# Rotation of 96 images by 90 degrees on one core: the last 16 MB of the loads move from SyncE's DMA queue to ScalarE's

## The chip, the core and the metric

The kernel runs on one core of one Trainium2 chip. The metric is the device time of one execution in microseconds (us). The core has compute engines of which two work here: VectorE (DVE in the profile) and ScalarE (ACT). SyncE (SP) computes nothing; it issues DMA transfers. Every transfer is cut up over the core's 16 DMA engines, whichever engine issued it.

## The reference

```python
def setup_inputs():
    batch, c, h, w = 32, 3, 256, 256
    return {"x": np.random.randn(batch, c, h, w).astype(np.float32)}

def reference(x):
    return np.rot90(x, k=-1, axes=(-2, -1)).astype(np.float32)
```

There are 96 images of 256 x 256 float32 numbers, and each is turned clockwise: row r of an image becomes a column. Nothing is calculated. 25.17 MB are read, 25.17 MB are written, and in between the numbers change places.

## The kernel before

All the data fit into the on-chip memory at once. They are split into five groups of 2, 2, 2, 4 and 2 slabs (`sizes`). One slab holds 128 partitions x 4096 numbers, that is 2048 KB, and in this text 1 MB is 1024 KB. Each group has one buffer `u0` to `u4` (all called u in the profile), in which its data are loaded, turned in place, and stored from. The whole kernel is straight-line code, and the order of the Python text is the order on each engine, as far as the waits between engines matter.

**Loads.** SyncE issues 14 of them, all on its one queue. They are numbered here from 0 in the order of issue:

- loads 0 and 1 (L55, 1 MB each) and load 2 (L56, 2 MB) bring group 0;
- loads 3 and 4 (L66, 2 MB each) bring group 1;
- loads 5 and 6 (L66) bring group 2;
- loads 7 to 10 (L66) bring group 3;
- load 11 (L66, 2 MB), load 12 (L63, 1 MB, named `mark`) and load 13 (L64, 1 MB) bring group 4.

The framework guards the transfers with eight semaphores, used in turn. So the issue of load k + 8 waits until load k has landed.

**Turning.** For each group VectorE makes transposes of 128 x 2048 numbers: L72 for group 0, and L88 and L93 for the others. A quarter or half of each group goes aside into `spare` or `extra` (L72, L88) while the rest moves inside u (L93). Then ScalarE copies the part that went aside back into u: two copies at L78 for group 0, and two to eight at L98 for each of the other groups. `turn_group` of group n needs all loads of that group.

**Stores.** SyncE issues ten of them, numbered here from 0: stores 0 and 1 (L106) for group 0, and two for each other group (L113): stores 2 and 3, 4 and 5, 6 and 7 (group 3, 4 MB each), 8 and 9. All others have 2 MB. A written-out dependence makes store 0 wait until load 12 (`mark`) has landed, so that practically all of the reading comes before all of the writing; the other stores follow on SyncE in order. Each waits for ScalarE's last copy of its group.

Functions that the change touches:

Of the kernel before, what the change touches and what calls it, by code (L numbers as in the profile page):

```python
# [1 line left out]

# [4 lines left out]


@with_exitstack  # L10
def kernel(
    ctx: ExitStack,
    tc: tile.TileContext,
    x: bass.AP,
    out: bass.AP,
):

    nc = tc.nc
    fp32 = mybir.dt.float32

    B, C, H, W = x.shape
    P = nc.NUM_PARTITIONS
    R = 16  # L30
    E = R * W
    hw = R // 2
    low, high = slice(0, hw), slice(hw, R)

    rows_in = x.rearrange("b c h w -> (b c h) w")
    rows_out = out.rearrange("b c h w -> (b c h) w")

    sizes = (2, 2, 2, 4, 2)
    first = [sum(sizes[:n]) for n in range(len(sizes))]
    groups = [  # L40
        ctx.enter_context(tc.tile_pool(name=f"group{n}", bufs=1)).tile([P, s, E], fp32, name=f"u{n}")
        for n, s in enumerate(sizes)
    ]
    psum = ctx.enter_context(tc.tile_pool(name="psum", bufs=1, space=bass.MemoryType.PSUM))
    spare = [psum.tile([P, E // 2], fp32, name=f"spare{h}") for h in range(2)]
    extra = ctx.enter_context(tc.tile_pool(name="extra", bufs=1)).tile([P, E // 2], fp32, name="extra")

    def rows_of(rows, n):
        return rows[first[n] * P * R : (first[n] + sizes[n]) * P * R]


    ld = rows_of(rows_in, 0).rearrange("(s i p r) w -> s i p (r w)", s=2, i=2, p=P)
    home = [groups[0][:, s].rearrange("p (i f) -> p i f", i=2) for s in range(2)]
    for i in range(2):
        nc.sync.dma_start(out=home[0][:, i], in_=ld[1, i])  # L55
    nc.sync.dma_start(out=home[1], in_=ld[0].transpose([1, 0, 2]))  # L56
    for n in range(1, len(sizes)):
        I = sizes[n]
        ld = rows_of(rows_in, n).rearrange("(a i m r) w -> i m a (r w)", a=2, i=I, m=P // I)
        to = groups[n].rearrange("p s f -> p (s f)").rearrange("p (a f) -> p a f", a=2)  # L60
        for i in range(I):
            if (n, i) == (len(sizes) - 1, I - 1):
                mark = nc.sync.dma_start(out=to[i::I, 0], in_=ld[i][:, 0])  # L63
                nc.sync.dma_start(out=to[i::I, 1], in_=ld[i][:, 1])  # L64
            else:
                nc.sync.dma_start(out=to[i::I], in_=ld[i])  # L66

    def turn_slab(src, dsts):
        s = src.rearrange("p (i r g c) -> p c r g i", i=2, r=R // 2, c=R)
        for h, d in enumerate(dsts):  # L70
            d = d.rearrange("p (c k r) -> p c r k", c=hw, r=R // 2)[:, :, ::-1, ::-1]
            nc.vector.transpose(out=d, in_=s[:, h * hw : (h + 1) * hw])  # L72

    u = groups[0]
    turn_slab(u[:, 0], spare)
    turn_slab(u[:, 1], [u[:, 0, : E // 2], u[:, 0, E // 2 :]])
    for h in range(2):
        nc.scalar.copy(out=u[:, 1, h * E // 2 : (h + 1) * E // 2], in_=spare[h])  # L78

    def turn_group(n, held):  # L80
        I = sizes[n]
        T = I // 2
        K = W // (R * T)
        u = groups[n].rearrange("p s f -> p (s f)")
        src = u.rearrange("p (a t r g c) -> p t c r g a", a=2, t=T, r=R, c=R)
        dst = u.rearrange("p (i c k t r) -> p t c r k i", i=I, c=R, k=K, t=T)[:, ::-1, :, ::-1, ::-1, :]
        for t in range(T):
            nc.vector.transpose(  # L88
                out=held[t].rearrange("p (i c k r) -> p c r k i", i=I, c=hw, k=K)[:, :, ::-1, ::-1, :],
                in_=src[:, t, low, low])  # L90
        for c, r in ((low, high), (high, high), (high, low)):
            for t in range(T):
                nc.vector.transpose(out=dst[:, t, c, r], in_=src[:, t, c, r])  # L93
        back = u.rearrange("p (i c k t r) -> p t i c k r", i=I, c=R, k=K, t=T)[:, ::-1]
        for t in range(T):
            kept = held[t].rearrange("p (i c k r) -> p i c k r", i=I, c=hw, k=K)
            for i in range(I):
                nc.scalar.copy(out=back[:, t, i, low, :, high], in_=kept[:, i])  # L98

    for n, held in enumerate(([extra], [spare[1]], spare, [extra]), 1):  # L100
        turn_group(n, held)


    st = rows_of(rows_out, 0).rearrange("(s i m r) w -> i m s (r w)", s=2, i=2, m=P // 2)
    for a in range(2):
        put = nc.sync.dma_start(out=st[a], in_=groups[0][a::2])  # L106
        if a == 0:
            tc.add_manual_dep(put.ins, mark.ins.name, mybir.DependencyInfo(
                mybir.DependencyClass.Sync, mybir.DependencyReason.SCHED_ONLY), reason="stores after loads")
    for n in range(1, len(sizes)):  # L110
        st = rows_of(rows_out, n).rearrange("(a i m r) w -> a m i (r w)", a=2, i=sizes[n], m=P // 2)
        for a in range(2):
            nc.sync.dma_start(out=st[a], in_=groups[n][a::2])  # L113


# [1 line left out]
_INS = ['x']  # L117
_OUTS = [((32, 3, 256, 256), 'float32')]


# [23 lines left out]
```

## Time and profile before

| | |
|---|---|
| median of 3 runs | 123.02 us (122.89 to 123.17) |
| the profiled execution | 122.88 us |
| its span in the profile | 121.1 us |
| VectorE busy | 87.4 us (72%), 24 instructions |
| ScalarE busy | 14.9 us (12%), 17 instructions |
| DMA | 50.33 MB (of a million bytes), mean 416 GB/s over the span |
| DMA queues in use | one (q1, from SyncE): 3456 packets, 97.6% of the 16 DMA engines' span |

The profile's times count from the start of the span. 1.78 us of the profiled execution lie outside of the span. A DMA issue is an instruction of its own on the issuing engine's sequencer (SPq for SyncE, ACTq for ScalarE); the profile gives the time it takes there, and apart from this the time from issue until the data have landed. The trace also keeps a record for each packet that a DMA engine moves: its start, its length and its size. Most packets here have 16 KB and there is one small packet at the end of each transfer on each DMA engine, which reports the landing.

### The profile page before, as it was taken

What the parts mean: (1) busy time and instruction counts of PE and PEld (TensorE: products, weight loads), DVE (VectorE), ACT (ScalarE), POOL (GpSimd) and SP (SyncE); (2) the same over time, 40 slices, a digit from 0 to 9 for tenths busy, and PEclk for the clock granted to TensorE, in tenths of its full rate; (3) what the DMA queues carried; (4) which work ended last, traced back from release to release, by engine and by line L of the source; (5) the groups of instructions that cost most, each with busy time, mean ns of one, the idle gap of its engine ahead of it and who ended that gap; (6) DMA issues with size and microseconds to landing.
All of it is one profiled execution on the core that took longest, in us unless ns stands there. A gap on an engine that the chain in (4) does not pass through costs nothing.

```text
span 121.1 us, 131 instructions
## 1 busy us (share of the span) xinstructions
DVE 87.4 (72%) x24; ACT 14.9 (12%) x17; POOL 0.2 (0%) x4
## 2 busy tenths in 40 slices
DVE  0039999999999999999999999999999600000000
ACT  0000400380005100060000000318000330000000
POOL 0000000000000000000000000000000000000000
DMA  2999999999989898999999999999999999999994
GB/s 89 428 428 422 452 433 433 433 433 433 520 346 520 346 520 346 428 422 411 433 433 428 433 433 428 417 417 433 428 433 433 433 433 433 433 433 433 433 422 184
DMA packets 3456, 50.33 MB, mean 416 GB/s; under 512 B 384, under 2 KB 384, under 8 KB 384
## 3 DMA queue, kind: packets, MB, share of 16 engines
q1 hardware_dynamic: 3456, 50.33, 97.6%
HBM read 25.17 MB, written 25.17 MB: 416 GB/s over the span
## 4 chain that ended last, share of the span: by engine, by line
DVE 66%; issue 6%; DMA 6%; ACT 1%; ACTq 1%; SPq 0%; DVEq 0%
DVE u L93 39%; DVE spare L88 9%; DVE extra L88 6%; DVE u L72 6%; DVE spare L72 6%; DMA u<-in_x_dram 6%; ACT u L98 1%; ACTq L139 1%; SPq L55 0%; DVEq L88 0%; DVEq L72 0%
## 5 line engine op out<-in xcount | busy, mean ns | idle before, releaser
L93 DVE STREAM_TRANSPOSE u<-u 128x2048 f32<-128x2048 f32 x15 | 54.4, 3649 | 0.4
L72 DVE STREAM_TRANSPOSE spare<-u 128x2048 f32<-128x2048 f32 x2 | 7.1, 3586 | 8.1 <-DMA u<-in_x_dram 8.1
L98 ACT COPY u<-spare 128x512 f32<-128x512 f32 (+1 forms) x10 | 6.0, 687 | 38.5 <-DVE u L93 38.5
L88 DVE STREAM_TRANSPOSE spare<-u 128x2048 f32<-128x2048 f32 x3 | 10.7, 3588 | 0.0
L72 DVE STREAM_TRANSPOSE u<-u 128x2048 f32<-128x2048 f32 x2 | 7.8, 3988 | 0.0
L88 DVE STREAM_TRANSPOSE extra<-u 128x2048 f32<-128x2048 f32 x2 | 7.8, 3896 | 0.0
L98 ACT COPY u<-extra 128x1024 f32<-128x1024 f32 x4 | 4.0, 1043 | 22.8 <-DVE u L93 22.8
L78 ACT COPY u<-spare 128x2048 f32<-128x2048 f32 x2 | 3.6, 1870 | 8.7 <-DVE u L72 8.7
L78 ACT ACT_TABLE_LOAD x1 | 1.3, 1283 | 13.0 <-DMA u<-in_x_dram 13.0
L128 POOL MEMSET const-uint8-127<- 128x1 uint8 x1 | 0.1, 103 | 0.0
L128 POOL MEMSET const-bfloat16-1.0<- 128x1 bf16 x1 | 0.1, 102 | 0.0
L128 POOL MEMSET const-float32-0.0<- 128x1 f32 x1 | 0.1, 99 | 0.2 <-issue 0.2
L128 POOL MEMSET const-float32-1.0<- 128x1 f32 x1 | 0.1, 99 | 0.0
## 6 DMA issues: line engine op xcount, KB each, us to landing
u<-in_x_dram SPq DMA_DIRECT2D x10, 2048.0 KB, 30.4
out_dram<-u SPq DMA_DIRECT2D x8, 2048.0 KB, 18.2
out_dram<-u SPq DMA_DIRECT2D x2, 4096.0 KB, 21.1
u<-in_x_dram SPq DMA_DIRECT2D x4, 1024.0 KB, 20.5
```

Of the source, the lines that this page charges most:

```text
L72: nc.vector.transpose(out=d, in_=s[:, h * hw : (h + 1) * hw])
L78: nc.scalar.copy(out=u[:, 1, h * E // 2 : (h + 1) * E // 2], in_=spare[h])
L88: nc.vector.transpose(out=held[t].rearrange("p (i c k r) -> p c r k i", i=I, c=hw, k=K)[:, :, ::-1, ::-1, :], in_=src[:, t, low, low])
L93: nc.vector.transpose(out=dst[:, t, c, r], in_=src[:, t, c, r])
L98: nc.scalar.copy(out=back[:, t, i, low, :, high], in_=kept[:, i])
L128: nc = _bacc.Bacc("TRN2", target_bir_lowering=False, num_devices=1)
L139: with _tile.TileContext(nc) as tc:
```

## The change

Loads 0 to 4 (8 MB) are still issued by SyncE. Loads 5 to 13 (16 MB) are put into a list `later` and issued by ScalarE on its own DMA queue. The first of them, load 5, gets a written-out dependence on load 3 (`early`), with which 6 MB have landed; the other eight follow in ScalarE's program order. `keep` fixes that order among the ScalarE instructions: loads 5 to 10, the two copies L78, loads 11, 12 and 13, and then the copies L98 of groups 1 to 4. `mark`, for which store 0 waits, is still load 12. The shapes of the transfers, the work of VectorE and the stores on SyncE stay as they are.

```diff
+    last = {}
+
+    def keep(inst):
+        before = last.get(inst.ins.engine)
+        if before is not None:
+            tc.add_manual_dep(inst.ins, before, ... NoSync, SCHED_ONLY ..., reason="order")
+        last[inst.ins.engine] = inst.ins.name
+        return inst
...
+    later = []
     for n in range(1, len(sizes)):
...
         for i in range(I):
-            if (n, i) == (len(sizes) - 1, I - 1):
-                mark = nc.sync.dma_start(out=to[i::I, 0], in_=ld[i][:, 0])
-                nc.sync.dma_start(out=to[i::I, 1], in_=ld[i][:, 1])
+            if n == 1:
+                got = nc.sync.dma_start(out=to[i::I], in_=ld[i])
+                if i == 0:
+                    early = got
+            elif (n, i) == (len(sizes) - 1, I - 1):
+                later += [(to[i::I, a], ld[i][:, a]) for a in range(2)]
             else:
-                nc.sync.dma_start(out=to[i::I], in_=ld[i])
+                later.append((to[i::I], ld[i]))
+
+    def load(k):
+        for o, i in later[k]:
+            got = keep(nc.scalar.dma_start(out=o, in_=i))
+            if "x" not in last:
+                last["x"] = None
+                tc.add_manual_dep(got.ins, early.ins.name, ... Sync, SCHED_ONLY ..., reason="loads in turn")
+        return got
...
+    load(slice(0, 6))
+
     u = groups[0]
     turn_slab(u[:, 0], spare)
     turn_slab(u[:, 1], [u[:, 0, : E // 2], u[:, 0, E // 2 :]])
     for h in range(2):
-        nc.scalar.copy(out=u[:, 1, h * E // 2 : (h + 1) * E // 2], in_=spare[h])
+        keep(nc.scalar.copy(out=u[:, 1, h * E // 2 : (h + 1) * E // 2], in_=spare[h]))
...
-                nc.scalar.copy(out=back[:, t, i, low, :, high], in_=kept[:, i])
+                keep(nc.scalar.copy(out=back[:, t, i, low, :, high], in_=kept[:, i]))
+
+    mark = load(slice(6, -1))
+    load(slice(-1, None))
```

More of the change, by code (lines that the diff above doesn't have):

```diff
@@ L49, in rows_of @@
         return rows[first[n] * P * R : (first[n] + sizes[n]) * P * R]
+    last = {}
+    def keep(inst):
+        before = last.get(inst.ins.engine)
+        if before is not None:
+            tc.add_manual_dep(inst.ins, before, mybir.DependencyInfo(
+                mybir.DependencyClass.NoSync, mybir.DependencyReason.SCHED_ONLY), reason="order")
+        last[inst.ins.engine] = inst.ins.name
+        return inst
     ld = rows_of(rows_in, 0).rearrange("(s i p r) w -> s i p (r w)", s=2, i=2, p=P)
@@ L61 @@
         for i in range(I):
-            if (n, i) == (len(sizes) - 1, I - 1):
-                mark = nc.sync.dma_start(out=to[i::I, 0], in_=ld[i][:, 0])
-                nc.sync.dma_start(out=to[i::I, 1], in_=ld[i][:, 1])
-            else:
-                nc.sync.dma_start(out=to[i::I], in_=ld[i])
+            if n == 1:
[4 more added lines that the diff above has]
+                later += [(to[i::I, a], ld[i][:, a]) for a in range(2)]
+            else:
+                later.append((to[i::I], ld[i]))
[4 more added lines that the diff above has]
+                last["x"] = None
+                tc.add_manual_dep(got.ins, early.ins.name, mybir.DependencyInfo(
+                    mybir.DependencyClass.Sync, mybir.DependencyReason.SCHED_ONLY), reason="loads in turn")
+        return got
     def turn_slab(src, dsts):
```

## Prediction

> **What bounds the kernel now.** I read the page first, for which resource is full.
>
> ```profile
> span 121.1 us, 131 instructions
> DVE 87.4 (72%) x24; ACT 14.9 (12%) x17; POOL 0.2 (0%) x4
> DMA  2999999999989898999999999999999999999994
> q1 hardware_dynamic: 3456, 50.33, 97.6%
> ```
>
> The only row that is full from edge to edge is DMA: its first slice has 2 tenths and its last has 4. VectorE stops at slice 32 of 40. The chain of waits names VectorE for most of the span, since it follows instructions backwards and ends in a store, but the stores stand in a queue. So I looked at the windows next.
>
> ```profile
> 20.00:40.00 20.00, 19.90 (x6) 5.63 (x4) 0.00 (x0) 1.00 1.01 433
> 40.00:60.00 20.00, 19.86 (x7) 1.93 (x2) 0.00 (x0) 1.00 1.00 430
> 60.00:80.00 20.00, 19.93 (x6) 1.07 (x2) 0.00 (x0) 1.00 1.00 429
> 80.00:100.00 20.00, 15.78 (x5) 5.02 (x8) 0.00 (x0) 1.00 1.00 425
> 100.00:119.00 19.00, 0.00 (x0) 0.00 (x0) 0.00 (x0) 1.00 1.01 428
> ```
>
> The last two columns are DMA share and GB/s: full in the load half (to 60 us), full in the store half, full when VectorE has ended. The trace's packet records say it more sharply. Chained into 16 engines, data packets run from 1.7 to 2.8 us (first ones) until 119.7 to 119.9 us, and no engine has a gap of 0.1 us in between, also not where load 13 gives way to store 0. A packet of 16 KB takes 611 to 619 ns; summed over a DMA engine, all packets together lie 0.80 us above the shortest of their size, 0.20 us of it before 3 us and 0.27 us in the loads from 3 to 60 us.
>
> So the time is 1.78 us outside of the span + about 2.3 us until the engines run + 117.4 us of packets + 1.3 us from the last packet to the end of the span = 122.8 us, against 122.88 us of the profiled execution. That execution lies 0.14 us under the median of 123.02 us, within the scatter of the three runs (0.28 us).
>
> Third view: SP's own waits (us in total, times, longest).
>
> ```profile
> SPq L106 <- DMA u<-in_x_dram: 31.2, 1, 31.2
> SPq L66 <- DMA u<-in_x_dram: 10.4, 3, 4.4
> SPq L113 <- ACT u L98: 5.0, 2, 3.0
> ```
>
> And three of its issues in the timeline (start, length in us).
>
> ```profile
> 17.84 0.61 SPq L66 DMA_DIRECT2D u<-in_x_dram  x1
> 59.43 1.37 SPq L106 DMA_DIRECT2D out_dram<-u  x2
> 84.25 15.73 SPq L113 DMA_DIRECT2D out_dram<-u  x4
> ```
>
> SP waits for its eight semaphores: load 11 goes out at 17.84, when load 3 has landed (17.82 in the trace), loads 12 and 13 at 22.75 and 27.64 when loads 4 and 5 have. All this runs some 30 us ahead of the data. Store 0 goes out at 59.43, when load 12 has landed. Store 6 goes out at 84.25, when group 3 is turned; its data are due only when store 5 is through, at 90.4 us.
>
> Fourth, the chain in order of time around the place that is touched:
>
> ```profile
> 15.18 7.60 DVE u L72 x2
> 22.78 0.06 issue
> 22.84 3.92 DVE extra L88
> ```
>
> VectorE is through with group 0 at 22.78 us, and load 4, which it needs next, landed at 22.73 us. It has no reserve there: every us by which load 4 is later is a us for VectorE, and VectorE never idles again before 95.9 us, so nothing absorbs it.
>
> **The change, part by part.** *Issues.* Nine issues leave SP (613 ns each by the median of L66, about 500 ns for L63 and L64). SP waits over 31 us for load 12 anyhow: no gain. On ScalarE they stand in line with its copies. Six issues from 17.84 on, 6 x 0.61 + 5 x 0.05 = 3.9 us, end at 21.7. The table load (1.28 us, at 13.0 before) may then end at 23.0, where the L78 copies start today (23.03, after VectorE). Copies until 26.7, loads 11 to 13 behind them by about 28.2 (load 13 has to wait for load 5's landing, about 27.6). Loads 5 to 10 last the queue until 51.5 us, and the next copy (L98 of group 1) is due at 37.7 us, so both sides have over 9 us of cover. Cost 0; VectorE needs `spare` back only at 37.6 us.
>
> *The hand-over.* Load 5's issue waits for load 3 (17.82 us). How long does ScalarE's idle queue take until packets move? The nearest row is the start of the kernel: issue at 0.73, first packets on four engines at 1.73 to 1.82 and on the other twelve at 2.39 to 2.79, so 1.0 to 2.06 us. That puts load 5 at 18.8 to 19.9 us. Load 4 alone keeps the engines busy until 22.2 us, 2.3 us longer. Cost 0; without that cover it would be the whole 1.0 to 2.06 us.
>
> *The shared stretch.* From about 19.3 us both queues have packets for every DMA engine. If they alternate one to one, the remaining 2.3 to 3.4 us of load 4 take twice as long. Its data end at 24.5 to 25.6, it lands 0.48 us later (as load 4 does today, 22.24 to 22.73), at 25.0 to 26.1 us, and VectorE is late by 2.2 to 3.3 us from there on. What is late next is store 6: issued at 86.5 to 87.6 instead of 84.25. It must go out 1.6 to 2.1 us (as long as store 0 and the head took) ahead of 90.4, so by 88.3 to 88.8 us: the reserve of 4.1 to 4.6 us holds by 0.7 to 2.3 us. Store 8 (97.93, due behind store 7 at 110 us) has over 10 us. Cost 0, on the thinnest cover of the sum.
>
> Alternation by one 16 KB packet is my reading of the packet records. The Trainium skill (DMA: Bandwidth & Descriptors, Queues, rings and completion order) says that a DMA engine goes round the queues by whole packets of typically 9 to 17 descriptors. By that rule load 4's eight pieces per engine could pass undivided, VectorE would not be late at all, and the time would be the same; no trace here shows two queues at work.
>
> *Switching between queues.* About 6 packets of load 4 per engine alternate with as many of load 5, and 4 of load 13 with store 0: some 14 switches. Nearest row: the change of direction from load 13 to store 0, where one packet took 634 ns and all others 611 to 618: 0 to 0.02 us each, 0 to 0.3 us in sum. From below: the whole excess in the load half is 0.27 us, so no overlap of two queues can bring more than that. I take 0, nearest to the change of direction.
>
> *Loads to stores.* Load 12's landing releases store 0 as before. Store 0's packets began 1.57 to 1.83 us after its issue (61.00 to 61.26), just behind load 13's. Then its queue was at work; now SyncE's queue has been empty for over 30 us. The idle start at the head of the kernel took up to 2.06 us on the late engines: 2.06 - 1.57 = 0.49 us of gap at worst, none at best, as the packets may have been ready early and stood in line. I take 0.1 us, nearer to the row of the store itself.
>
> *Around the span.* One queue more at launch and end has no row. The nearest is the wait of the preamble's barrier, 0.7 us (SPq <- PEq L128); I take 0 and keep 0.7 us as the upper end, and 0 as the lower, since nothing is removed there.
>
> Sum: 122.88 + 0.1 = 122.98 us in the profiled execution, or 123.02 + 0.1 = 123.1 us against the median. The bytes, the 16 engines and the moments at which the first load and the first store are released stay.
>
> The Trainium skill (same page, Rules for kernel authors) speaks against any gain: spreading DMAs over issuing engines saves only issue time, since all run on the same 16 engines. The packets without gaps agree, and by the rule the sum would be 123.0.
>
> **The rivals.** *Unequal shares (slower).* ScalarE's queue holds six loads, SyncE's holds one. If the engines serve ScalarE's queue twice for each packet of load 4, its last 2.3 to 3.4 us take three times as long, it lands at 27.3 to 29.5, and store 6 goes out at 88.8 to 91.0 instead of by 88.3 to 88.8 at the latest. The engines then stand still: 0 to 2.7 us, in the middle 1.4 us, so 124.4. It decides as soon as load 4 lands later than about 27.1 us, and from there each us costs a us. For it: no reserve at 22.78 us. Against it: nothing in the trace shows a preference.
>
> *Idle-queue costs (slower).* Store 0's gap (0.49 us) or a cost at launch (up to 0.7), or 0.02 us per switch (0.3): some 0.5 us, 123.5. For it: store 0 had just come in time. Against it: the late engines at the head also waited for the very first data.
>
> *Faster.* Two queues close the packets' excess, in the load half and where load 13 meets store 0: -0.27 us, 122.75. Against it: there is no gap to fill, and in some 50 of the 57 us only one queue is at work.
>
> *The change does not hold its wait.* If load 5 went out at 0.7 us, both queues would share from the start; the 8 MB would land near 40 instead of 22.7 us, VectorE would be late by 17 us, store 6 by 13 us beyond its reserve: 136. The dependence is written out, so this is remote.
>
> **How the numbers follow.** About 0.25 us (0.2%) is what a measurement of this kernel can tell from no change. My forecast, no change within that, has 0.50; its own range is 122.8 to 123.25. Idle-queue costs 0.21, unequal shares 0.10, the lost wait 0.02, which makes slower 0.33. Faster 0.17. The range reaches from 122.6 (the whole -0.27 and 0.1 of scatter) to 124.2: 123.02 + 0.49 + 0.3 + 0.4, most of the idle-queue costs together and the lower half of the unequal shares; beyond it lie about 0.1 above and 0.07 below.
>
> **What would show it.** Right: a second queue with 16.8 of the 50.33 MB; ScalarE's first issue near 17.8 us; DMA at 9 tenths in all slices but first and last; L88 of group 1 starting at 25 to 26 us instead of 22.84; store 0 still at 59.4 and store 6 at 86.5 to 87.6 us; the span within 0.3 us. Wrong: a slice at 90 us with DMA under 9 tenths (store 6 late), a dip at 19 to 25 or at 61 us (switches, idle queue), 16 KB packets of other length than 611 to 619 ns, or a landing of load 12 away from 59.3 us. A time under 122.75 would mean that packets have become shorter or that the ends outside of the stream have, which I do not see.

## The result and the profile after

The changed kernel takes 152.94 us (152.71 to 153.04) against 123.0 us: 1.2427 times as long, with a 95% interval of 1.2412 to 1.2442. The forecast of 123.1 us lies 29.8 us below that, and the upper end of its range, 124.2 us, 28.7 us.

The page of the changed kernel first: span, VectorE's and DMA's busy tenths in 40 slices (3.78 us each), and the two queues.

```profile
span 151.2 us, 133 instructions
DVE  0089999999200006999999999999995000000000
DMA  4999999999999999999999990000000199999996
q1 hardware_dynamic: 2544, 33.56, 52.6%
q10 hardware_dynamic: 912, 16.78, 26.4%
```

Three things are to be seen. The second queue is there with its 16.78 MB. VectorE has a hole of some four slices, from about 38 to 58 us. And DMA, the resource that was full from edge to edge, stands still for seven slices, from about 91 to 120 us. The windows say that outside of that hole it is as fast as ever (the last two columns are DMA share and GB/s):

```profile
60.00:90.00 30.00, 29.90 (x9) 1.93 (x2) 0.00 (x0) 1.00 1.01 429
91.00:120.00 29.00, 24.54 (x7) 5.01 (x10) 0.00 (x0) 1.00 0.00 0
121.00:149.00 28.00, 0.00 (x0) 0.00 (x0) 0.00 (x0) 1.00 1.01 430
```

So the 30 us are not made of slower transfers. In the hole the DMA engines had nothing to do. What they waited for is in SP's waits (us in total, times, longest):

```profile
SPq L144 <- DVE u L121: 42.2, 2, 35.7
```

and in its issues in the timeline (start, length):

```profile
27.57 0.65 SPq L137 DMA_DIRECT2D out_dram<-u  x1
119.12 4.09 SPq L144 DMA_DIRECT2D out_dram<-u  x4
```

Store 6, the first of group 3, goes out at 119.1 us instead of 84.2, because VectorE is through with group 3 only at 115.5 us and ScalarE's copies follow. And a store has slipped in among the loads, at 27.57 us: store 1, which nothing ties to `mark`. (`mark` holds back store 0 alone. Before, store 1 stood behind it.) Now VectorE in the order of time, from group 1 on:

```profile
23.47 3.92 DVE L116 STREAM_TRANSPOSE extra<-u 128x2048 f32<-128x2048 f32 x1 [0.34 <-DMA u<-in_x_dram]
27.42 11.18 DVE L121 STREAM_TRANSPOSE u<-u 128x2048 f32<-128x2048 f32 x3
57.84 7.08 DVE L116 STREAM_TRANSPOSE spare<-u 128x2048 f32<-128x2048 f32 x2 [19.24 <-DMA u<-in_x_dram]
64.95 10.93 DVE L121 STREAM_TRANSPOSE u<-u 128x2048 f32<-128x2048 f32 x3
75.78 3.87 DVE L116 STREAM_TRANSPOSE extra<-u 128x2048 f32<-128x2048 f32 x1
79.49 3.53 DVE L116 STREAM_TRANSPOSE spare<-u 128x2048 f32<-128x2048 f32 x1
82.93 32.61 DVE L121 STREAM_TRANSPOSE u<-u 128x2048 f32<-128x2048 f32 x9
```

And before, from group 2 on:

```profile
37.60 3.59 DVE L88 STREAM_TRANSPOSE spare<-u 128x2048 f32<-128x2048 f32 x1
41.23 10.93 DVE L93 STREAM_TRANSPOSE u<-u 128x2048 f32<-128x2048 f32 x3
52.12 7.08 DVE L88 STREAM_TRANSPOSE spare<-u 128x2048 f32<-128x2048 f32 x2
59.23 21.92 DVE L93 STREAM_TRANSPOSE u<-u 128x2048 f32<-128x2048 f32 x6
81.04 3.88 DVE L88 STREAM_TRANSPOSE extra<-u 128x2048 f32<-128x2048 f32 x1
84.96 10.93 DVE L93 STREAM_TRANSPOSE u<-u 128x2048 f32<-128x2048 f32 x3
```

Before, `spare` was written once after group 1 (group 2), then three L93 followed, then `spare` twice (group 3), then six L93, and `extra` (group 4) came last of the four. Here `spare` is written twice in a row, `extra` comes before the last `spare`, and nine L121 follow at the end. Which group an instruction belongs to can be read from the trace, although all buffers are called u: a transpose of group 3 writes in the pattern 4 x 8 x 8 x 8, one of groups 1, 2 and 4 in 2 x 16 x 8 x 8. VectorE's instructions stand in another order:

```
before:  group 1 | group 2: aside, 3 moves | group 3: aside, aside, 6 moves | group 4: aside, 3 moves
after:   group 1 | group 3: aside | group 2: aside, 3 moves | group 4: aside | group 3: aside
         | then three times: 1 move of group 4, 2 moves of group 3
```

("Aside" is L116, into `spare` or `extra`; a move is L121.) The first transpose of group 3 needs all of loads 7 to 10, and so VectorE sits idle for 19.24 us with group 2 lying ready. At the end groups 3 and 4 are turned side by side, so that group 3, whose stores come first, is finished with VectorE's last instruction.

In numbers, all from the two traces: VectorE ends at 115.5 instead of 95.9 us, 19.6 more; group 3 is done at its end instead of 14.8 us earlier; the copies behind it take 0.5 us more. That is 34.9 us for store 6 (84.25 to 119.12). The spans differ by 30.1 us (151.2 - 121.1), so 4.8 us were hidden: the reserve of store 6, which the table at the end of the experiments shows for other runs too.

### The profile page after: what moved, and what is told of

Read it like the earlier page. It is cut to its first block, busy times and chain, and to the rows that moved or that the text cites. A ratio compares the mean times of both kernels' runs of the same rounds, so it can differ in the third digit from the quotient of the medians.

```text
span 151.2 us, 133 instructions
## 1 busy us (share of the span) xinstructions
DVE 87.5 (58%) x24; ACT 14.8 (10%) x17; POOL 0.2 (0%) x4
## 3 DMA queue, kind: packets, MB, share of 16 engines
q10 hardware_dynamic: 912, 16.78, 26.4%
## 4 chain that ended last, share of the span: by engine, by line
DMA 34%; DVE 31%; issue 5%; ACT 3%; ACTq 3%; DVEq 3%; SPq 1%
DMA u<-in_x_dram 34%; DVE u L121 24%; DVE spare L116 5%; ACT u L126 3%; DVE extra L116 3%; DVEq L170 2%; ACTq L87 2%; ACTq L170 1%; SPq L67 1%; SPq L68 0%; DVEq L116 0%
## 5 line engine op out<-in xcount | busy, mean ns | idle before, releaser
L121 DVE STREAM_TRANSPOSE u<-u 128x2048 f32<-128x2048 f32 x15 | 54.6, 3691 | 0.2
L116 DVE STREAM_TRANSPOSE spare<-u 128x2048 f32<-128x2048 f32 x3 | 10.6, 3566 | 19.2 <-DMA u<-in_x_dram 19.2
L98 DVE STREAM_TRANSPOSE spare<-u 128x2048 f32<-128x2048 f32 x2 | 7.1, 3585 | 8.2 <-DMA u<-in_x_dram 8.2
L116 DVE STREAM_TRANSPOSE extra<-u 128x2048 f32<-128x2048 f32 x2 | 7.8, 3892 | 0.3 <-DMA u<-in_x_dram 0.3
L98 DVE STREAM_TRANSPOSE u<-u 128x2048 f32<-128x2048 f32 x2 | 7.8, 3988 | 0.0
```

The source lines that it names most:

```text
L116: nc.vector.transpose(out=held[t].rearrange("p (i c k r) -> p c r k i", i=I, c=hw, k=K)[:, :, ::-1, ::-1, :], in_=src[:, t, low, low])
```

## The experiments

Three theories stood at the start. A: the changed order on VectorE and SyncE is the cause, and the second queue costs nothing by itself. B: the second queue is the cause. C: the early store is. Later, for the parts of the order, D and E, and F for the parts of the edit.

**Order written out again.** The diff's own `keep` put around VectorE's transposes and around the stores of the changed kernel, and nothing else.

```diff
-            nc.vector.transpose(out=d, in_=s[:, h * hw : (h + 1) * hw])
+            keep(nc.vector.transpose(out=d, in_=s[:, h * hw : (h + 1) * hw]))
...
-                nc.vector.transpose(out=dst[:, t, c, r], in_=src[:, t, c, r])
+                keep(nc.vector.transpose(out=dst[:, t, c, r], in_=src[:, t, c, r]))
...
-            nc.sync.dma_start(out=st[a], in_=groups[n][a::2])
+            keep(nc.sync.dma_start(out=st[a], in_=groups[n][a::2]))
```

> The changed kernel, with its order written out for VectorE (all transposes in the order of the text: group 1, 2, 3, 4) and for the stores on SyncE (store 0 before store 1), as the change already does for ScalarE. Loads 5 to 13 stay on ScalarE's queue. Theory A (the order of the instructions on VectorE and SyncE, which came out differently, costs the 30 us; the second queue costs nothing): 122.9 to 123.5 us, no stretch with DMA at 0, store 6 issued at 84 to 88 us. Theory B (the second queue itself costs the time: loads on it land late or share unfairly): above 130 us, and VectorE still idle for over 10 us before group 2 or 3.

Measured: 123.0 us, ratio 1.0001 to the kernel before (0.9992 to 1.001). Its page:

```profile
span 121.1 us, 132 instructions
DMA  4999999999989898999999999999999999999994
```

The span is that of the kernel before to the tenth, with 16.78 MB on the second queue. Store 6 went out at 85.30 us. Theory A holds, and B falls: all of the 30 us come from the order.

**VectorE's order alone written out**, so that store 1 may still slip in.

> The changed kernel with VectorE's order alone written out; store 1 may still go ahead of store 0, at about 27.6 us among the loads. Theory A: group 3's loads end 4.9 us later than before (57 instead of 52 us), VectorE idles about 5.5 us there, store 6 goes out at about 90 us; the five stores ahead of it still fill the engines until about 91, so 123.0 to 124.0 us. Theory B: above 130 us.

Measured: 124.32 us, ratio 1.0104 (1.0089 to 1.012), 0.3 us over what was expected. VectorE waits once more:

```profile
DVE spare L116 <- DMA u<-in_x_dram: 5.1, 1, 5.1
```

Store 6 went out at 90.53 us, 1.5 us behind the limit of 89.05 us that the table below gives. With VectorE's order right, the early store costs 1.3 us.

**The stores' order alone written out.**

> The changed kernel with the order of the stores alone written out; VectorE keeps its changed order (a quarter of group 3 ahead of group 2, groups 3 and 4 interleaved). Theory A: group 3's loads land at about 52 instead of 57.6 us, so VectorE idles about 14 us instead of 19.2 and ends at about 110 us, store 6 goes out at about 114 us, and the whole takes 147 to 149 us. If the early store mattered most (theory C), it would fall to below 130 us.

Measured: 147.32 us, ratio 1.1979 (1.1957 to 1.2001), VectorE idle 13.8 us, store 6 at 113.36 us. Theory C falls. With VectorE's order wrong, the early store had cost 5.6 us (152.94 - 147.32), since there no reserve was left to hide any of it.

**The kernel before, with VectorE's order of the changed one.** All loads on SyncE's queue; `turn_group` is cut into its parts, and these are called, and kept, in the other order:

```diff
-    for n, held in enumerate(([extra], [spare[1]], spare, [extra]), 1):
-        turn_group(n, held)
+    whole(g1)
+    g3[0](0)                # aside
+    whole(g2)
+    g4[0](0)
+    g3[0](1)
+    for q in range(3):
+        g4[1](q)            # moves
+        g3[1](q)
+    g3[2]()                 # copies
+    g4[2]()
```

> The kernel before, all loads on SyncE's queue, with nothing changed but VectorE's order, which is written out as the changed kernel has it. Theory A: VectorE waits from 37.6 to 52 us for group 3's loads (14.3 us) and ends at 110.2 us with group 3's last quarter; store 6 goes out 3.6 us later at 113.8, its packets start at 115.5 instead of 90.4 us: 25 us more, 148 us. Theory B: within 1 us of the kernel before, 123 us, as only one queue is used.

Measured: 147.22 us, ratio 1.1971 (1.1949 to 1.1993), the same within 0.1 us as the changed kernel with its stores in order. One queue or two made no difference to it.

```profile
span 145.4 us, 131 instructions
DMA  4999999999999999999999998000000599999995
```

And its longest wait of VectorE behind the first load:

```profile
DVE spare L101 <- DMA u<-in_x_dram: 14.4, 1, 14.4
```

The hole in DMA and the wait of VectorE are back with a single queue. (ScalarE's copies are not kept here, and the framework put group 4's two copies ahead of group 3's though the text has them behind. That is the same freedom once more.)

**Each half of the order by itself**, again in the kernel before. The swap: group 3's first aside ahead of group 2, the rest in order.

> The kernel before with one difference in VectorE's order: the first transpose of group 3 stands ahead of group 2. Theory A: it needs all loads of group 3, so VectorE idles from 37.6 to about 52 us (14.4 us); everything behind it moves by that: store 6 goes out at 98.6 instead of 84.25, its packets start 1.7 us later at 100.3 instead of 90.4, so 9.9 us more: 132.9 us. If an early quarter of group 3 costs nothing by itself (theory D: only the interleaving does), 123 us.

Measured: 134.81 us (ratio 1.0959, 1.0927 to 1.0991), 1.9 us over what was expected. The rows of VectorE's waits say why:

```profile
DVE spare L101 <- DMA u<-in_x_dram: 14.5, 1, 14.5
DVE spare L101 <- ACT u L114: 2.0, 1, 2.0
```

The second wait was not in the sum: group 3's second aside goes into the half of `spare` that group 2 has just used, and directly behind group 2 it has to wait for ScalarE's two copies out of it.

The interleaving: groups 1 and 2 in order, then groups 3 and 4 side by side.

> The kernel before with the other difference in VectorE's order: groups 3 and 4 interleaved, quarter by quarter, group 2 ahead of both. Theory A: VectorE never idles and ends at 95.9 us as before, but now with group 3's last quarter instead of group 4's; ScalarE's copies follow and store 6 goes out at 99.5 instead of 84.25 us, packets at 101.2 instead of 90.4: 10.8 us more, 133.8 us. Theory D: 148 us less what the swap costs. If the wait for group 3's loads were all (theory E), 123 us.

Measured: 138.98 us (ratio 1.1299, 1.1266 to 1.1331), 5.2 us over.

```profile
DVE extra L101 <- DMA u<-in_x_dram: 6.1, 1, 6.1
```

Group 4's first transpose has moved forward to 55.9 us, and waits there until 62.0 us for group 4's loads. So both halves cost, 11.8 and 16.0 us; D and E fall. Together they cost 24.2 and not 27.8 us: after the swap's wait neither of the two extra waits (2.0 and 6.1 us) arises, but store 6's reserve of 4.8 us is taken off once and not twice.

**One word.** In the changed kernel `nc.scalar.dma_start` becomes `nc.sync.dma_start` for loads 5 to 13. The list, the wait for load 3 and `keep` stay.

> The changed kernel with one word different: loads 5 to 13 are issued by SyncE instead of ScalarE, still as a list, with the wait for load 3 ahead of load 5 and with the written-out order. No order is written out for VectorE or the stores. Theory A with the queue as the trigger: VectorE's order stays that of the kernel before, and so does the time, 122.9 to 123.4 us. If the list or the wait for load 3 changes the order (theory F): near 150 us.

Measured: 122.97 us, ratio 0.9997 (0.9985 to 1.0008). The order on VectorE and SyncE is that of the text again: stores 0 and 1 go out one behind the other at 59.54 and 60.26 us, and VectorE puts groups 2, 3 and 4 aside in turn.

```profile
37.72 3.59 DVE L116 STREAM_TRANSPOSE spare<-u 128x2048 f32<-128x2048 f32 x1
52.24 7.08 DVE L116 STREAM_TRANSPOSE spare<-u 128x2048 f32<-128x2048 f32 x2
81.36 3.89 DVE L116 STREAM_TRANSPOSE extra<-u 128x2048 f32<-128x2048 f32 x1
```

Theory F falls: the list and the wait do not turn the order by themselves; it turns when ScalarE issues the loads. One thing goes along with the word, though. `keep` goes by engine: with the loads on ScalarE it ties them and the copies into one row, with the loads on SyncE it ties the loads and the copies each by themselves. Whether the engine or this tie turns VectorE's order was not tried apart.

**How two queues share.** The step of the prediction with the thinnest cover was the stretch with both queues. With the order written out, the wait ahead of load 5 was moved: to load 2 (4 MB), to load 1 (2 MB), and taken away.

```diff
-                if i == 0:
-                    early = got
...
-    nc.sync.dma_start(out=home[1], in_=ld[0].transpose([1, 0, 2]))
+    early = nc.sync.dma_start(out=home[1], in_=ld[0].transpose([1, 0, 2]))
```

> The changed kernel with VectorE's and the stores' order written out, and with load 5 waiting for load 2 (4 MB landed, 13.0 us) instead of load 3. ScalarE's packets take 3.6 to 4 us from the issue, as with the wait for 6 MB (17.9 to 21.5), so they start at 16.7 to 17.1 us, where load 4 begins; load 4's eight packets per engine then alternate with load 5's and it lands at 27.4 to 28.0 instead of 22.7 us. VectorE is late by 4.6 to 5.2 us, store 6 goes out at 88.8 to 89.4, against 88.3 to 88.8 at the latest: a gap of 0 to 1.1 us, 123.0 to 124.1 us. If two queues do not share before the first is empty: 123.0 and load 4 landing at 22.7 to 23.4.

> The same with load 5 waiting for load 1 (2 MB landed, 8.0 us). ScalarE's packets start at 11.7 to 12.1 us; loads 3 and 4 share with loads 5 and 6 packet by packet, and load 4 lands at 32.3 to 32.9 us. VectorE is late by 9.5 to 10.1 us, store 6 goes out at 93.8 to 94.4, 5.0 to 6.1 us past the reserve: 128.0 to 129.1 us. If two queues do not share before the first is empty: 123.0.

For the third, the dependence of load 5 is left out altogether; each load still has a buffer of its own.

> The changed kernel with VectorE's and the stores' order written out, and without the wait for 6 MB: ScalarE issues load 5 at the start of the kernel, at the same time as SyncE issues load 0. If the two queues alternate packet by packet (8 KB of group 0 against 16 or 32 KB of groups 2 and 3), loads 0 and 1 land near 10 and 17 instead of 5.5 and 8 us, load 2 near 42 instead of 13, loads 3 and 4 near 52 instead of 23; VectorE is late by 29 us, store 6 goes out near 113: about 148 us. If a DMA engine first drains what was queued first, 123 to 126 us.

Measured: 124.06 us (1.0083, 1.0066 to 1.0099) for the wait for 4 MB, 130.83 us (1.0634, 1.0612 to 1.0655) for 2 MB, 151.46 us (1.2312, 1.2277 to 1.2348) without. What VectorE waited for load 4, in this order (in the third the lower two rows are its waits for loads 0 and 1 and for load 2):

```profile
DVE extra L114 <- DMA u<-in_x_dram: 5.3, 1, 5.3
```

```profile
DVE extra L114 <- DMA u<-in_x_dram: 12.0, 1, 12.0
```

```profile
DVE extra L116 <- DMA u<-in_x_dram: 16.6, 1, 16.6
DVE spare L98 <- DMA u<-in_x_dram: 13.3, 1, 13.3
DVE u L98 <- DMA u<-in_x_dram: 11.1, 1, 11.1
```

The two queues do alternate piece by piece (a piece is one data packet of the trace): without the wait, each of the 16 DMA engines moves from 6 to 19 us one 8 KB piece of SyncE's queue (309 ns) and one 16 KB piece of ScalarE's (611 ns) in turn, 16 of each per 0.92 us over all engines. The smaller pieces get a third of the bytes, and they belonged to the group that was needed first. The first result lies at the upper end of what was expected, the second 1.7 us above it and the third 3.5 us, and each time load 4 landed later than computed: at 28.4 instead of 27.4 to 28.0 us, at 35.0 instead of 32.3 to 32.9, at 55.8 instead of 52. In the trace the small packet that reports the landing stands in turn with the other queue as well, and on the slowest DMA engine it comes behind one more of its pieces. With the wait for 2 MB these were load 7's pieces of 32 KB by then, where the expectation had reckoned with 16 KB.

**All in one table.** Where store 6 goes out and how long the span is, from the traces:

| kernel | store 6 issued, us | span, us | span less store 6 |
|---|---|---|---|
| before | 84.25 | 121.1 | 36.8 |
| changed, order written out | 85.30 | 121.1 | 35.8 |
| changed, loads 5 to 13 on SyncE, order not written out | 85.07 | 121.2 | 36.1 |
| changed, order written out, wait for 4 MB | 90.29 | 122.3 | 32.1 |
| changed, VectorE's order written out | 90.53 | 122.6 | 32.1 |
| changed, order written out, wait for 2 MB | 96.89 | 128.9 | 32.0 |
| before, swap | 101.01 | 133.0 | 32.0 |
| before, interleaving | 105.17 | 137.2 | 32.1 |
| changed, stores in order | 113.36 | 145.4 | 32.0 |
| before, both | 113.39 | 145.4 | 32.1 |
| changed, order written out, no wait | 117.63 | 149.7 | 32.0 |
| changed | 119.12 | 151.2 | 32.0 |

In the lower nine rows, with one queue and with two, the last column lies between 32.04 and 32.06 us before rounding. So from 89.05 us on (121.1 - 32.05) each us by which store 6 was late was a us of the time. Whatever made it late, no other cost over 0.1 us is left to find.

## Why the prediction was wrong

**What held.** The kernel before is bound by its packets, and the second queue by itself brought and cost nothing (ratio 1.0001 with the order written out). That it was to bring nothing had been read from the packets without gaps, and the Trainium skill (DMA: Bandwidth & Descriptors, Rules for kernel authors) says so too; the run with the order written out agrees with both. The hand-over without a gap held, though not by its reckoning (see the terms below). Store 0 after the idle queue held as well: issued at 59.52 us, packets at 60.9 to 61.3, right behind load 13's, so that of the 0.49 us at worst and the 0.1 us taken, 0 was paid. Switches and the launch of a second queue cost 0. Store 6 as what is late next, and a limit of 88.3 to 88.8 us for it, held within 0.3 us: the runs give 89.05. Even its sign of being wrong came, DMA under 9 tenths at 90 us because store 6 is late; but load 4 was the only thing that it let delay store 6.

**The step that failed.** It is the path from load 4 to store 6 in the shared stretch: load 4 late, VectorE "late by 2.2 to 3.3 us from there on", store 6 "issued at 86.5 to 87.6 instead of 84.25", "Cost 0". It takes for granted that the instructions of VectorE and SyncE stand in the order of the text. The introduction says so ("the order of the Python text is the order on each engine"), and so does the account of the change ("the work of VectorE and the stores on SyncE stay as they are"). No row was given for this term, and it is not so. What the runs showed in its place: VectorE had a transpose of group 3 ahead of group 2 and idled 19.24 us for it, finished group 3 with its last instruction, and store 6 went out at 119.12 us. The moment at which the first store is released, which the sum says stays, moved too: store 1 went out at 27.57 us. With the order written out the 30 us were gone. The framework arranges the instructions of each engine itself, within what the data demand. In the kernel before, its arrangement happened to be the text's. With the loads on ScalarE it came out differently. `keep` held ScalarE's order and nothing else; VectorE and the stores were left free. All four rivals inherited the premise, and so none of them had the case.

There was a sign in the diff: it writes out an order for ScalarE, which would be needless if the text gave the order. The right question would have been which engines had no order written out, and what the worst legal order on them would cost. The price of one such order can be worked out from the trace of before alone: group 3's loads landed at 51.9 us, group 2 was begun at 37.6, so a swap makes VectorE 14.3 us late, against a reserve of 4.1 to 4.6 us.

**Terms that were mis-sized.** In the shared stretch, load 4 was to land 2.2 to 3.3 us late by one-to-one sharing. It landed 0.65 to 0.72 us late (23.38 to 23.45 us, in the four runs with this hand-over), as the queues hardly shared: load 5, issued at 17.93 in the run with the order written out, had its first packets at 21.9 to 22.3 us, when load 4's last pieces had gone. On 5 of the 16 DMA engines one of them went ahead of load 4's small closing packet, and these 0.61 us are most of the delay. The 1.0 to 2.06 us taken from the head of the kernel were too short for a queue that starts beside a busy one, and of the 2.3 us of cover at most one piece (0.61 us) was left, or load 5 would have taken turns with load 4, as it did in the runs with an earlier start. That the hand-over still cost nothing was in part luck. The Trainium skill's rule (DMA: Bandwidth & Descriptors, Queues, rings and completion order), by which a DMA engine passes on only after a packet of typically 9 to 17 descriptors, is not tested by this hand-over. If a piece in the trace is one descriptor, the runs with an earlier start do not fit that rule: there the engines changed after every single piece.

The rival in which the wait is lost was put at 136 us; the run without it took 151.46. Its term was load 4 at "near 40" us: it landed at 55.8, because pieces of 8 KB took turns with pieces of 16 and 32 KB.

**What stays open.** Why the framework's arrangement turns when the loads change engines is not seen in any trace; that this one word turns it is shown, but not whether by the engine or by what `keep` then ties together. Why a queue's first packets take 4 us and more beside a busy one is not settled either.

## What to carry to other kernels

In this framework, moving instructions to another engine can rearrange engines that the edit doesn't touch, so an engine whose order matters needs it written out, and a profile after such an edit is read first for the order of the operations and only then for their durations. Where transfers are the bound, look for the transfer with the smallest reserve behind the compute engines (here store 6, with 4.8 us): up to it a delay was free here, and beyond it each us counted in full. The second DMA queue added no bandwidth in these runs, and what it carried competed piece by piece with the load that was needed next. So look at when it may start: here the wait for 6 MB was free, for 4 MB it cost 0.8%, for 2 MB 6.3%, and no wait 23%.

## What the runs showed of the hardware that was not expected

- A transfer issued on an idle queue while the other queue was busy got its first packet 4.0 to 4.4 us later: with the order written out, load 5 issued at 17.93, packets from 21.9 us; with the wait for 4 MB 13.15 and 17.3; for 2 MB 8.07 and 12.0; without a wait 0.73 and 4.9; store 1 of the changed kernel 27.57 and 31.9. Where the other queue was about to run out (store 0 at 59.52 us) it took 1.4 to 1.8 us. (The 3.6 to 4 us in two of the expectations had been read from rows of half a us.)
- Two busy queues alternated by pieces and not by bytes: without the wait, 8 KB against 16 KB, later 16 KB against 32 KB (611 and 1213 ns). The total stayed near 420 to 430 GB/s, and the queue with pieces of twice the size got twice the rate.
- While store 1 starts up among the loads of the changed kernel, 34 of load 6's 16 KB packets take 0.67 to 1.17 instead of 0.61 us between 29.4 and 33.2 us, 0.8 us per DMA engine in sum (0.9 us with VectorE's order alone written out, where store 1 goes out early as well, and nothing where it does not). The window around it:

```profile
28.00:32.00 4.00, 3.97 (x2) 0.00 (x0) 0.00 (x0) 1.00 1.00 344
```
